# Two hyena gate tiles move into an attention head, where they share a seven-product pair

## The chip, the cores and the metric

The kernel runs on one core of a Trainium2 chip. The metric is the device time of one execution in microseconds. Three runs of the kernel before gave 885.85, 886.38 and 887.53 us, so a median of 886.38 us.

## What is computed

One layer of a hybrid backbone on 640 tokens (128 prompt tokens and 512 latent tokens) of 1024 channels, in float32. The modulated input `h` is multiplied by a wide projection `w_in`, whose columns feed two branches. Cut to what matters here:

```python
hy, g_h, qkv, g_a, m = split(h @ w_in)          # 3072, 1024, 3072, 1024, 2048 columns
v_h, x1, x0 = split(short_conv(hy))             # three groups of channels, three taps each
u   = v_h * x1
y_h = (irfft(rfft(u) * rfft(filter)) + u * d_bias) * x0        # hyena branch
y_a = attention(q, k, v)                                       # attention branch
p_h = (y_h * silu(g_h)) @ w_bh
p_a = (y_a * silu(g_a)) @ w_ba
out = (sigmoid(m_h) * p_h + sigmoid(m_a) * p_a) @ w_out
x_new = layer_norm(ALPHA * x + gate * out)
```

The change concerns `silu(g_h)` for the first 256 of the 1024 hyena channels. The kernel computes `silu(z)` as `(tanh(z/2) + 1) * z`; the missing factor 1/2 is taken into later constants.

## The kernel before

Everything is channel-major: a tile has 128 channels on the partitions and the 640 tokens along the free side, in two halves of 320. Every float32 matrix is split into a high part and a low part of the type fp32r, and a product is three matmuls (high by high, high by low, low by high). An output tile of 128 channels from 1024 inputs is therefore 8 blocks of inputs x 3 products x 2 halves = 48 matmuls of 320 columns (`proj`, `accumulate`, L168).

The program has these stages, in order of time:

1. Prologue: modulation, `h` in high and low parts (`hH`, `hL`), the filter network.
2. Hyena stage, in four quarters of two channel tiles (rows `n` = 2q and 2q+1). `quarter_head(q)` makes `v_h` and `x1` of the two rows, that is four projection tiles with their short convolution (`conv_tile`). `quarter_tail(q)` makes for each of the two rows a tile `x0` (`conv_tile`) and a gate tile `g_h` (`gate_tile`, weights 24 to 31). `long_conv` and `long_conv_back` do the transforms: small matmuls on TensorE with much VectorE work between them. `weave(main, side, n_main, n_side)` interleaves the projections (main) with the transforms and the next filter spectrum (side) in proportion to the two counts; one full quarter has eight projection tiles, `8 * NK` steps.
3. The row `yh` of the hyena branch is `silu(g_h) * x0 * u`. `gapped_product` multiplies and at the same time brings the token order of the convolution (image rows) into the order of the attention (column blocks). When both factors are there, `gate_conv` multiplies by `u` and stores the row to DRAM (`yh_d`).
4. Attention, eight pairs of heads `j` = 0 to 7 (called heads here). Each head has four steps of scores, softmax and values (`attend`), woven into projections for later heads (`mains`). From head 1 on these projections are made in pairs of output tiles by `pair_tile`: a two-by-two block product with seven instead of eight block multiplications, on sums of the weights (`prepare`, L1033) and sums of `h` (`token_sums`). A pair is 7 products x 4 blocks x 3 = 84 matmuls of 320 columns (L1068). `pair_tile` hands out the four quarters of the result in the order (1,1), (0,0), (1,0), (0,1), as (tile, half), by a callback `use`. `follow` says which pair's weights are prepared while a pair is computed. In head 1 the pairs are `mix(0)` and `queries_keys(3)`, in head 2 `mix(1)`, `queries_keys(4)` and `gates_a(2)`.
5. Output: the rows `yh` come back from DRAM (`yh_raw`, the first ones in head 7), are split, and go through `w_bh`, `w_ba`, the merge, `w_out` and the layer norm.

What sets the order: each engine runs its instructions in the order of its queue. In the attention stage TensorE's order is that of the program text. Everywhere else, and on the other engines throughout, a scheduler that plays the program on assumed durations chooses the order at build time. Loads are issued by SyncE's queue (`nc.sync`, SPq), some stores by ScalarE's (`nc.scalar`), and in the hyena stage the low part of a weight is made by an accumulating DMA from GpSimd's queue (L148). The ring of prepared weights `wb` has two buffers of one tag and three of another, raw weights have two.

Of the kernel before, what the change touches and what calls it, by code (L numbers as in the profile page):

```python
# [18 lines left out]
NK = 8  # L19
# [26 lines left out]
def tile_hyena_natten_step(ctx: ExitStack, tc: tile.TileContext, a, o):  # L46
# [424 lines left out]
    def gapped_product(y, x):  # L471
        nc.vector.tensor_tensor(y[:, :LP], y[:, :LP], x[:, :LP], op=ALU.mult)
        xs, yb = by_row(x[:, GAP:NG]), y[:, SC : SC + LS]
        for b0, n, src in ((0, 1, xs[:, :, 7:8]), (1, 7, xs[:, :, 0:7])):
            ys = from_blocks(yb[:, 64 * b0 : 64 * (b0 + n)], n)
            nc.vector.tensor_tensor(ys, ys, src, op=ALU.mult)

    def conv_tile(i, dst):
        lo, hi = yield from proj(i, eng="dma")
        convw = out["convw"]  # L480
        zs = zss[0]
        zss.reverse()
        nc.scalar.activation(zs[:, 1 : 1 + LP], lo[:, :LP], AF.Copy)
        nat = by_row(zs[:, GAP + 1 : NG + 1])
        nc.scalar.activation(nat[:, :, 7:8], from_blocks(lo[:, B7], 1), AF.Copy)
        nc.scalar.activation(nat[:, :, 0:2], from_blocks(lo[:, B01], 2), AF.Copy)
        nc.scalar.activation(nat[:, :, 2:7], from_blocks(hi[:, :HALF], 5), AF.Copy)
        d = dst[:, :NG]
# [40 lines left out]
    def quarter_tail(q):  # L529
        yh = out["yh"]  # L530
        for i in range(2):
            n = 2 * q + i
            x0 = hwa.tile([P, NG + 1], F32, tag="cv", bufs=2, name=f"x0_{n}")
            yield from conv_tile(16 + n, x0)
            yield
            yh[n] = row(yhp, "yh", f"yh{n}")
            yield from gate_tile(24 + n, yh[n][:], "dma")
            gapped_product(yh[n], x0)
            gate_conv(n)
            yield  # L540

# [132 lines left out]
    pinned[0] = False  # L674
    for q in range(3):
        weave(chain(quarter_head(q + 1), quarter_tail(q)), chain(long_conv(q), braid(long_conv_back(q), filter_spectrum(q + 1))),
              8 * NK, N_CONV + N_BACK + N_FILTER)
    ident = out["ident"]

    def rows(h):  # L680
# [371 lines left out]

    def pair_tile(i0, i1, use):
        def halfrow(tag, bufs, name):
            return sp.tile([P, 384], F32, tag=tag, bufs=bufs, name=f"{name}{i0}")[:, :HALF]

        if i0 not in ready:
            prepare(i0, i1, False)
        wb, prep = ready.pop(i0)
        ps = {}  # L1060
        for j in range(7):
            if j < 4:
                ps["xyvz"[j]] = acc(f"sp{i0}_{j}")[:, :HALF]
            dst, x = ps["xyvzxvz"[j]], operand(ORDER[j])
            for k in range(4):
                wh, wl = (wb[j][:, i, P * k : P * k + P] for i in range(2))
                for i, (wk, xi) in enumerate(((wh, 0), (wh, 1), (wl, 0))):
                    nc.tensor.matmul(  # L1068
                        dst, wk, x(xi, k), start=j < 4 and k == 0 and i == 0, stop=k == 3 and i == 2, skip_group_check=True,
                    )  # L1070
                if k == 1:
                    yield
            if j == 0:
                u = halfrow("u", 1, "u")
                nc.scalar.activation(u, dst, AF.Copy)
            elif j == 1:
                nc.vector.tensor_tensor(u, dst, u, op=ALU.add)
            elif j == 4:
                use(0, 0, dst)
            else:  # L1080
                if j != 3:
                    c = halfrow("c", 4, f"c{j}_")
                nc.vector.tensor_tensor(c, dst, c if j == 3 else u, op=ALU.add)
                if j != 2:
                    use(*{3: (1, 1), 5: (1, 0), 6: (0, 1)}[j], c)
            prep(j + 5)
            if j == 3 and (i0, i1) in follow:
                prepare(*follow[i0, i1], True)
            yield
# [5 lines left out]
    def gates_a(j):  # L1095
# [7 lines left out]

        yield from pair_tile(T_GA + j, T_GA + j + 1, use)

    def mix(m):
        t0, dst = (T_MH, mh_d) if m < 4 else (T_MA, ma_d)
        n0 = 2 * (m % 4)

        def use(i, hf, src):  # L1110
            th = sp.tile([P, 384], F32, tag="c", bufs=4, name=f"th{m}")[:, :HALF] if hf == i == 0 else src
# [13 lines left out]
    def mix_(m):  # L1125
        t = (T_MH if m < 4 else T_MA) + 2 * (m % 4)
        return t, t + 1

    runs = (
        (mix_(0), qk_(3), mix_(1), qk_(4), ga_(2)), (mix_(2), qk_(5), mix_(3), ga_(4), qk_(6)),  # L1130
        (mix_(4), qk_(7), mix_(5), ga_(6), mix_(6), mix_(7)),
    )
    follow = {x: y for run in runs for x, y in zip(run, run[1:])}
# [45 lines left out]
    def mains(j):  # L1179
        return {  # L1180
            0: ((alongside(chain(gate_a(1), queries(2), keys(2)), token_sums(1), 2, 5),), 3 * NK),
            1: ((mix(0), queries_keys(3)), 2 * N_PAIR),
            2: ((mix(1), queries_keys(4), gates_a(2)), 3 * N_PAIR),
            3: ((values(2), mix(2)), N_VALUES + N_PAIR),
            4: ((queries_keys(5), mix(3), gates_a(4)), 3 * N_PAIR),
# [327 lines left out]
```

## Time and profile before

| what | value |
|---|---|
| median of three runs | 886.38 us (885.85 to 887.53) |
| profiled execution: its time, and its span | 885.91 us, 884.1 us |
| TensorE (PE) busy, weight loads (PEld) busy | 872.7 us, 844.7 us |
| VectorE (DVE), ScalarE (ACT), GpSimd (POOL) busy | 635.2, 429.4, 127.4 us |
| granted TensorE clock | 0.997 of full speed on average |
| matmuls | 6532 |

A row of the group view gives the source line, the engine, the operation, the tile written and the tiles read, then the busy time and the mean duration of one, then the idle time of the engine just before it and what ended it. Matmuls overlap: one of 320 columns is shown as 310 ns long, though the next starts sooner. A row of the time line gives the start, the length and how many alike were merged. A row of the chain of waits gives the start, the length of the piece and what ran in it.

The attention stage begins near 387 us of the span and ends near 706 us.

### The profile page before, as it was taken

What the parts mean: (1) busy time and instruction counts of PE and PEld (TensorE: products, weight loads), DVE (VectorE), ACT (ScalarE), POOL (GpSimd) and SP (SyncE); (2) the same over time, 40 slices, a digit from 0 to 9 for tenths busy, and PEclk for the clock granted to TensorE, in tenths of its full rate; (3) what the DMA queues carried; (4) which work ended last, traced back from release to release, by engine and by line L of the source; (5) the groups of instructions that cost most, each with busy time, mean ns of one, the idle gap of its engine ahead of it and who ended that gap; (6) DMA issues with size and microseconds to landing.
All of it is one profiled execution on the core that took longest, in us unless ns stands there. A gap on an engine that the chain in (4) does not pass through costs nothing.

```text
span 884.1 us, 16779 instructions
## 1 busy us (share of the span) xinstructions
PE 872.7 (99%) x6532; PEld 844.7 (96%) x6532; DVE 635.2 (72%) x1257; ACT 429.4 (49%) x912; POOL 127.4 (14%) x128
## 2 busy tenths in 40 slices
PE   8999999999999999999999999999999999999996
PEld 7899999999999999999999999999999999999885
DVE  5776693795679478699787567865877667676666
ACT  4395454645445432356665465555655632243200
POOL 0010110010101000024423322222222200000000
PEclk9999999999999999999999999999999999999998
DMA  9975666656656231253525153434252488545611
GB/s 351 381 165 131 140 136 123 140 136 142 141 118 137 71 108 55 72 195 104 164 80 168 55 153 99 142 105 124 78 181 80 135 304 279 165 157 195 212 62 57
DMA packets 53834, 129.07 MB, mean 146 GB/s; under 512 B 8283, under 2 KB 23131, under 8 KB 53756
## 3 DMA queue, kind: packets, MB, share of 16 engines
q1 hardware_dynamic: 44108, 107.72, 37.4%
q0 software_dynamic: 4032, 14.68, 10.2%
q10 hardware_dynamic: 5616, 5.61, 1.9%
q8 instruction: 51, 0.84, 0.4%
q14 instruction: 27, 0.22, 0.1%
HBM read 113.83 MB, written 14.16 MB: 145 GB/s over the span
## 4 chain that ended last, share of the span: by engine, by line
PE 94%; DVE 3%; DMA 1%; ACT 1%; issue 0%; POOL 0%; POOLq 0%; DVEq 0%; ACTq 0%
PE mm L168 38%; PE sp L1068 19%; PE mm L182 6%; PE out L1328 6%; PE v L769 5%; PE pt L866 2%; PE s L873 2%; PE s L826 2%; PE ve L781 1%; DMA raw<-wall 1%; PE adaT L249 1%; DVE wb L102 1%; DVE s L1033 1%; PE adaT L266 1%; PE fl L401 1%; PE yb L158 1%
## 5 line engine op out<-in xcount | busy, mean ns | idle before, releaser
L1068 PE MATMUL sp<-t,wb 128*128 128x320 f32 x768 | 120.6, 310 | 0.0
L168 PE MATMUL mm<-hH,wh 128*128 128x320 f32 x480 | 114.6, 313 | 0.9 <-ACT hH L329 0.7
L1068 PEld LDWEIGHTS sp<-t,wb 128*128 128x128 f32 x768 | 113.8, 188 | 0.5 <-issue 0.5
L168 PE MATMUL mm<-hL,wh 128*128 128x320 f32 x480 | 113.0, 311 | 0.0
L168 PE MATMUL mm<-hH,wl 128*128 128x320 f32 x480 | 112.1, 310 | 0.4 <-DVE wl L102 0.4
L1068 PE MATMUL sp<-hH,wb 128*128 128x320 f32 x384 | 93.2, 313 | 0.0
L168 PEld LDWEIGHTS mm<-hH,wh 128*128 128x128 f32 x480 | 80.7, 188 | 3.3 <-issue 1.4
L168 PEld LDWEIGHTS mm<-hL,wh 128*128 128x128 f32 x480 | 80.9, 188 | 1.1 <-DVE hL L330 0.5
L168 PEld LDWEIGHTS mm<-hH,wl 128*128 128x128 f32 x480 | 80.8, 188 | 0.8 <-DVE wl L102 0.7
L1068 PEld LDWEIGHTS sp<-hH,wb 128*128 128x128 f32 x384 | 66.1, 188 | 1.9 <-issue 1.9
L101 ACT ACTIVATE wh<-raw 128x1024 fp32r<-128x1024 f32 x33 | 34.8, 1058 | 60.4 <-PE mm L168 29.1
L848 POOL TENSOR_SCALAR p<-p,sm 128x384 f32<-128x384 f32 x32 | 47.6, 1497 | 108.7 <-DVE sm L847 76.2
L148 POOL DMA_DIRECT2D wl<-wall x28 | 24.4, 871 | 259.3 <-ACT wl L147 232.2
L1068 PE MATMUL sp<-hL,wb 128*128 128x320 f32 x192 | 59.3, 309 | 0.0
L102 DVE TENSOR_TENSOR wb<-s,wb 128x512 fp32r<-128x512 f32 x64 | 43.7, 695 | 16.7 <-ACT wb L101 16.7
L149 ACT ACTIVATE wh<-raw 128x1024 fp32r<-128x1024 f32 x28 | 29.7, 1062 | 50.6 <-PE mm L168 50.6
L101 ACT ACTIVATE wb<-s 128x512 fp32r<-128x512 f32 x64 | 39.0, 628 | 30.0 <-DVE s L1033 24.5
L102 DVE TENSOR_TENSOR wl<-raw,wh 128x1024 fp32r<-128x1024 f32 x33 | 40.2, 1220 | 12.1 <-ACT wh L101 11.9
L1328 PE MATMUL out<-woh,yhs 128*128 128x512 f32 (+1 forms) x176 | 45.5, 372 | 0.0
L101 ACT ACTIVATE wb<-raw 128x512 fp32r<-128x512 f32 x48 | 30.1, 627 | 31.2 <-PE sp L1068 17.3
L848 POOL TENSOR_SCALAR edge<-edge,sm 128x320 f32<-128x320 f32 x32 | 43.6, 1373 | 1.9 <-DVE sm L847 1.9
L102 DVE TENSOR_TENSOR wb<-raw,wb 128x512 fp32r<-128x512 f32 x48 | 33.4, 697 | 12.6 <-ACT wb L101 11.7
(357 smaller groups left out, 2164.5 us busy)
## 6 DMA issues: line engine op xcount, KB each, us to landing
raw<-wall SPq DMA_DIRECT2D x95, 512.0 KB, 3.7
wl<-wall POOLq DMA_DIRECT2D x28, 512.0 KB, 5.6
ada<-wada SPq DMA_DIRECT2D x16, 512.0 KB, 8.3
tm<-bias SPq DMA_DIRECT2D x16, 512.0 KB, 4.5
gate<-wgate SPq DMA_DIRECT2D x8, 512.0 KB, 3.9
wo<-wall SPq DMA_DIRECT2D x8, 512.0 KB, 4.2
xt<-xT SPq DMA_DIRECT2D x8, 320.0 KB, 7.8
dec<-decay SPq DMA_DIRECT2D x20, 128.0 KB, 3.4
```

What stands on the lines that cost most here:

```text
L101: hi = nc.scalar.activation(dst_h, src, AF.Copy)
L102: return hi, (eng or nc.vector).tensor_tensor(dst_l, src, f(dst_h), op=ALU.subtract)
L148: nc.gpsimd.dma_start(wl, a["wall"][i], accum_op=ALU.add)
L149: nc.scalar.activation(wh, raw[:], AF.Copy)
L168: nc.tensor.matmul(ps[hf][:, :HALF], wt[k], x[:, hf * HALF : (hf + 1) * HALF], start=(i == 0 and k == 0), stop=(i == lead[2] and k == NK - ...
L182: nc.tensor.matmul(p[:, :HALF], w[i // 2][k], (hH, hL)[i % 2][:, k, cs], start=n == 0, stop=n == len(steps) - 1, skip_group_check=True,)
L769: nc.tensor.matmul(ps[t // 2][:, t % 2 * 256 : t % 2 * 256 + 256], x[:, k, P * t : P * t + P], wk, start=first and t % 2 == 0, stop=last, ...
L826: nc.tensor.matmul(dst[h], x[rows(h), qs], y[rows(h), ks], start=i == 0, stop=i == 2, skip_group_check=True)
L848: nc.gpsimd.tensor_scalar_mul(pv, pv, sm[:, 2:3])
L866: nc.tensor.transpose(pt[:, i * P : i * P + P], x, ident)
L1068: nc.tensor.matmul(dst, wk, x(xi, k), start=j < 4 and k == 0 and i == 0, stop=k == 3 and i == 2, skip_group_check=True,)
L1328: ins = nc.tensor.matmul(dst, m[k][:, c0 : c0 + P], w[:, c : c + n], start=(first and k == 0), stop=(last and k == 5), skip_group_check=True,)
```

## The change

- For rows 0 and 1, both of quarter 0, the gate tile leaves `quarter_tail`. In its place `natural` copies `x0` into the row in the new token order, three ScalarE copies. The row that `gate_conv` stores to `yh_d` is then `x0 * u`, without its gate.
- The two gate tiles are made together as one pair in head 1, after `mix(0)` and `queries_keys(3)`, by `gates_h`. Its callback takes each half row of 320 tokens from DRAM (two buffers, tag `yg`), multiplies it by `z`, makes `tanh(z/2)`, adds one and multiplies, and stores the half row to its place in `yh_d` from ScalarE's queue. The half rows three and four are fetched into the buffers of the first two after these have been stored.
- The main count of quarter 0's weave goes from 64 to 48 steps, that of head 1 from 28 to 42, and `follow` gets the new pair between `queries_keys(3)` and `mix(1)`.
- Half-row scratch tiles are 320 instead of 384 columns wide.

```diff
+    def natural(y, x):
+        nc.scalar.activation(y[:, :LP], x[:, :LP], AF.Copy)
+        xs, yb = by_row(x[:, GAP:NG]), y[:, SC : SC + LS]
+        for b0, n, src in ((0, 1, xs[:, :, 7:8]), (1, 7, xs[:, :, 0:7])):
+            nc.scalar.activation(from_blocks(yb[:, 64 * b0 : 64 * (b0 + n)], n), src, AF.Copy)
...
-            yield from gate_tile(24 + n, yh[n][:], "dma")
-            gapped_product(yh[n], x0)
+            if n in (0, 1):
+                natural(yh[n], x0)
+            else:
+                yield from gate_tile(24 + n, yh[n][:], "dma")
+                gapped_product(yh[n], x0)
...
-              8 * NK, N_CONV + N_BACK + N_FILTER)
+              (8 - sum(n // 2 == q for n in (0, 1))) * NK, N_CONV + N_BACK + N_FILTER)
...
-            return sp.tile([P, 384], F32, tag=tag, bufs=bufs, name=f"{name}{i0}")[:, :HALF]
+            return sp.tile([P, HALF], F32, tag=tag, bufs=bufs, name=f"{name}{i0}")[:]
...
+    def gates_h(*ns):
+        order = ((1, 1), (0, 0), (1, 0), (0, 1))
+        ys = {}
+
+        def fetch(k):
+            if k < 4:
+                i, hf = order[k]
+                ys[k] = at.tile([P, HALF], F32, tag="yg", bufs=2, name=f"yg{ns[i]}_{hf}")
+                nc.sync.dma_start(ys[k][:], yh_d[ns[i]][:, CS[hf]])
+
+        def use(i, hf, src):
+            k = order.index((i, hf))
+            y = ys[k][:]
+            th = sp.tile([P, HALF], F32, tag="c", bufs=4, name=f"gh{ns[0]}")[:] if hf == i == 0 else src
+            nc.vector.tensor_tensor(y, y, src, op=ALU.mult)
+            nc.scalar.activation(th, src, AF.Tanh, scale=0.5)
+            nc.vector.scalar_tensor_tensor(y, th, 1.0, y, op0=ALU.add, op1=ALU.mult)
+            nc.scalar.dma_start(yh_d[ns[i]][:, CS[hf]], y)
+            fetch(k + 2)
+
+        fetch(0)
+        fetch(1)
+        yield from pair_tile(24 + ns[0], 24 + ns[1], use)
...
-        (mix_(0), qk_(3), mix_(1), qk_(4), ga_(2)), (mix_(2), qk_(5), mix_(3), ga_(4), qk_(6)),
+        (mix_(0), qk_(3), gh_(0), mix_(1), qk_(4), ga_(2)), (mix_(2), qk_(5), mix_(3), ga_(4), qk_(6)),
...
-            1: ((mix(0), queries_keys(3)), 2 * N_PAIR),
+            1: ((mix(0), queries_keys(3), gates_h(*GH[0])), 3 * N_PAIR),
```

How the order moves. VectorE, before, where head 1 hands over to `mix(1)`, the first pair of head 2 (`wb` are prepared weights of `mix(1)`, `s` sums of raw weights, `kl` low parts of keys, `c` half rows of the pair's result):

```order
L102 TENSOR_TENSOR wb_2_5278<-s_66_5268,wb_2_5278 128x512
L1033 TENSOR_TENSOR s_66_5270<-raw_5264,s_66_5270 128x512
L741 TENSOR_TENSOR kl_5259<-c_35_5346,k_5258 128x64
L741 TENSOR_TENSOR kl_5259<-c_35_5346,k_5258 128x128
L1033 TENSOR_TENSOR s_66_5281<-raw_5266 128x512
L741 TENSOR_TENSOR kl_5259<-c_35_5346,k_5258 128x128
L1083 TENSOR_TENSOR c_35_5370<-sp_3_5244,u_5207 128x320
L102 TENSOR_TENSOR wb_4_5287<-raw_5264,wb_4_5287 128x512
L102 TENSOR_TENSOR wb_3_5284<-s_66_5281,wb_3_5284 128x512
```

The low parts of keys of `queries_keys(3)` stand between the weights of `mix(1)`; none of these instructions reads what a DMA has just fetched, but for the raw weights. VectorE at the same handover with the change (`yg` are the half rows fetched from DRAM, `smp` and `yo` belong to the attention step):

```order
L1092 TENSOR_TENSOR c_24_5401<-sp_3_5306,u_5245 128x320
L102 TENSOR_TENSOR wb_2_5340<-s_66_5330,wb_2_5340 128x512
L1042 TENSOR_TENSOR s_66_5332<-raw_5326,s_66_5332 128x512
L1129 TENSOR_TENSOR yg_0_5324<-yg_0_5324,c_24_5383 128x320
L102 TENSOR_TENSOR wb_4_5349<-raw_5326,wb_4_5349 128x512
L1042 TENSOR_TENSOR s_66_5343<-raw_5328 128x512
L1129 TENSOR_TENSOR yg_1_5369<-yg_1_5369,c_24_5401 128x320
L902 TENSOR_REDUCE smp_5457<-s_0_5414 128x1
L902 TENSOR_REDUCE smp_5457<-s_1_5415 128x1
L1131 SCALAR_TENSOR_TENSOR yg_0_5324<-c_24_5383,yg_0_5324 128x320
L923 TENSOR_TENSOR yo_5444<-sg_4388,s_0_5416 128x128
L102 TENSOR_TENSOR wb_3_5346<-s_66_5343,wb_3_5346 128x512
```

The products of the third and fourth half row (`yg_0_5324`, `yg_1_5369`), which wait for their fetch, now stand ahead of the weights `wb_4` and `wb_3` of `mix(1)`. SyncE's queue with the change, at that place:

```order
L748 DMA new_kT<-c_35_5200 128x128
L63 DMA tm_5487<-bias 128x1024
L63 DMA tm_5489<-bias 128x1024
L63 DMA raw_5326<-wall 128x1024
L63 DMA raw_5328<-wall 128x1024
L1123 DMA yg_0_5324<-yh_d 128x320
L1123 DMA yg_1_5369<-yh_d 128x320
L63 DMA raw_5550<-wall 128x1024
```

The two late fetches come behind the raw weights of `mix(1)` (5326, 5328) and ahead of those of `queries_keys(4)` (5550); before, two bias loads (`tm`) and one store stood between them. ScalarE in quarter 0 with the change, where before the gate's two `tanh` (L501) stood:

```order
L147 ACTIVATE wl_1817<-raw_1814 128x1024
L495 ACTIVATE x_1_1496<-zs_104,pack_373 128x641
L419 ACTIVATE F_1172<-fa_1173 128x2x256
L479 ACTIVATE yh_1482<-x_0_1357 128x128
L482 ACTIVATE yh_1482<-x_0_1357 128x64
L482 ACTIVATE yh_1482<-x_0_1357 128x8x7x8
L101 ACTIVATE sh_2_1207<-sd_2_1205 128x512
```

The three copies of `natural` (L479, L482) take the place of the two `tanh` and of one gate tile's two weight copies. From head 2's second pair on, the order on every engine is as before.

More of the change, by code (lines that the diff above doesn't have):

```diff
@@ L1110, in use @@
         def use(i, hf, src):
-            th = sp.tile([P, 384], F32, tag="c", bufs=4, name=f"th{m}")[:, :HALF] if hf == i == 0 else src
+            th = sp.tile([P, HALF], F32, tag="c", bufs=4, name=f"th{m}")[:] if hf == i == 0 else src
             nc.scalar.activation(th, src, AF.Tanh, scale=0.5)
@@ L1127, in mix_, with gh_ @@
         return t, t + 1
+    GH = ((0, 1), ())
+    def gh_(m):
+        return 24 + GH[m][0], 24 + GH[m][1]
     runs = (
-        (mix_(0), qk_(3), mix_(1), qk_(4), ga_(2)), (mix_(2), qk_(5), mix_(3), ga_(4), qk_(6)),
+        (mix_(0), qk_(3), gh_(0), mix_(1), qk_(4), ga_(2)), (mix_(2), qk_(5), mix_(3), ga_(4), qk_(6)),
         (mix_(4), qk_(7), mix_(5), ga_(6), mix_(6), mix_(7)),
```

## The prediction

> **What bounds the kernel now.** First the page's busy times, with the granted clock and the shares of the chain of waits that ended last.
>
> ```profile
> span 884.1 us, 16779 instructions
> PE 872.7 (99%) x6532; PEld 844.7 (96%) x6532; DVE 635.2 (72%) x1257; ACT 429.4 (49%) x912; POOL 127.4 (14%) x128
> PEclk9999999999999999999999999999999999999998
> PE 94%; DVE 3%; DMA 1%; ACT 1%; issue 0%; POOL 0%; POOLq 0%; DVEq 0%; ACTq 0%
> ```
>
> TensorE is busy 99% of the span at full clock and holds 94% of the chain. Busy alone can hide gaps, since matmuls overlap; so next the view of waits, TensorE's own, which is complete with these five rows.
>
> ```profile
> PE adaT L266 <- POOL spare L281: 1.5, 1, 1.5
> PE mm L168 <- ACT hH L329: 0.7, 1, 0.7
> PE mm L168 <- DVE wl L102: 0.4, 1, 0.4
> PE mm L168 <- ACT wh L101: 0.2, 1, 0.2
> PE adaT L249 <- DVE arg L219: 0.2, 1, 0.2
> ```
>
> That is 3.0 us, all in the prologue. Third, the chain in order of time (start, length, what), for what one matmul really costs in either place of the change: the length of a piece over its count is the distance between starts.
>
> ```profile
> 278.46 10.12 PE mm L168 x69
> 541.21 9.67 PE sp L1068 x66
> ```
>
> 10.12/69 and 9.67/66 give 146.7 and 146.5 ns: a projection matmul of 320 columns costs the same in the hyena stage (L168) and in a pair (L1068). Last, the stages that the change touches, by windows: quarters 0 and 1 of the hyena stage, head 1 and head 2.
>
> ```profile
> 83.00:164.00 81.00, 81.00 (x574) 80.54 (x573) 55.25 (x90) 43.75 (x82) 7.78 (x9) 1.00 0.62 135
> 164.00:244.00 80.00, 80.00 (x566) 79.54 (x565) 55.68 (x89) 42.81 (x82) 7.78 (x9) 1.00 0.61 134
> 411.30:445.00 33.70, 33.70 (x279) 32.52 (x278) 28.82 (x81) 23.00 (x65) 11.27 (x10) 1.00 0.41 131
> 445.00:491.00 46.00, 46.00 (x363) 44.82 (x362) 35.31 (x95) 28.01 (x69) 14.62 (x10) 1.00 0.43 129
> ```
>
> After each window's length come PE, PEld, DVE, ACT and POOL. TensorE is full in all four; VectorE, the next, has 55 of 81 us in quarter 0 and 29 of 34 in head 1. So what the change does to the number of matmuls is time, and what it does on the other engines is time only where a result comes too late for TensorE.
>
> **The change part by part.** *TensorE.* Two gate tiles leave: 2 x 48 = 96 matmuls. One pair comes: 84. The transforms, scores and values keep their counts, and so do the transposes that stand alone in the stream. The net is 12 matmuls less, 12 x 0.1467 = 1.76 us (14.08 out, 12.32 in).
>
> [...]
>
> *Other engines in quarter 0.* The durations:
>
> ```profile
> L147 ACT ACTIVATE wl<-raw 128x1024 fp32r<-128x1024 f32 x28 | 30.0, 1072 | 0.0
> L501 ACT ACTIVATE yh<-mm 128x320 f32<-128x320 f32 x16 | 6.0, 426 | 0.0
> L496 DVE SCALAR_TENSOR_TENSOR yh<-yh,mm 128x320 f32<-128x320 f32 x16 | 7.1, 480 | 0.0
> L476 DVE TENSOR_TENSOR yh<-yh,x 128x64 f32<-128x64 f32 (+1 forms) x16 | 6.3, 418 | 0.0
> L472 DVE TENSOR_TENSOR yh<-yh,x 128x128 f32<-128x128 f32 x8 | 2.3, 283 | 0.0
> ```
>
> VectorE loses four gate products and the two rows' products with x0: 4 x 0.48 + 4 x 0.42 + 2 x 0.28 = 4.2 us. ScalarE loses 4 weight copies (1.07 each) and 4 tanh, 6.0 us, and gains six small copies, bounded by the tanh at 0.43 each: 2.6 us. Two raw loads and two accumulating loads leave their queues, and come back as the pair's two raw loads. All of it lies beside TensorE, so I cost it at nothing. The cover: quarter 0 shrinks to 81 - 14.1 = 66.9 us, with 55.25 - 4.2 = 51 us of VectorE work, 76% against 68% before. The tight place is the spectrum product, where TensorE has only projections to run between the last matmul on `p_X` and the first on `yb`. By the order of instructions these are 163 with the change against 176 in quarter 0; quarter 1 got by with 139 before (20.4 us) and did not wait, and with the change quarters 1 and 2 have 152 and 164. Were the cover gone, each missing projection matmul would be 0.147 us of wait.
>
> *Other engines in head 1.* The pair's VectorE work, in rows of the same operations:
>
> ```profile
> L102 DVE TENSOR_TENSOR wb<-s,wb 128x512 fp32r<-128x512 f32 x64 | 43.7, 695 | 16.7 <-ACT wb L101 16.7
> L1033 DVE TENSOR_TENSOR s<-raw,raw 128x512 f32<-128x512 f32 x16 | 11.2, 703 | 8.2 <-DMA raw<-wall 8.2
> L1083 DVE TENSOR_TENSOR c<-sp,u 128x320 f32<-128x320 f32 x48 | 23.2, 484 | 13.6 <-PE sp L1068 13.6
> L496 DVE SCALAR_TENSOR_TENSOR sg<-sg,c 128x320 f32<-128x320 f32 x9 | 4.4, 485 | 0.5 <-ACT sg L1101 0.5
> ```
>
> Four sums and seven low parts (11 x 0.70), five result additions, four products and four gates (13 x 0.484): 14.0 us, brought by a pair that is 12.3 us on TensorE. Head 1 then has at most 28.8 + 14.0 = 42.8 us of VectorE work in 46.0 us, 93%: still under TensorE, so again nothing, as long as the order has no late place. The latest is the handover to `mix(1)`. Before, on VectorE's and TensorE's time lines:
>
> ```profile
> 443.84 0.68 DVE L102 TENSOR_TENSOR wb<-s,wb 128x512 fp32r<-128x512 f32 x1
> 444.44 0.69 DVE L1033 TENSOR_TENSOR s<-raw,s 128x512 f32<-128x512 f32 x1
> 446.18 0.48 DVE L1083 TENSOR_TENSOR c<-sp,u 128x320 f32<-128x320 f32 x1
> 446.58 0.68 DVE L102 TENSOR_TENSOR wb<-raw,wb 128x512 fp32r<-128x512 f32 x1
> 447.18 0.68 DVE L102 TENSOR_TENSOR wb<-s,wb 128x512 fp32r<-128x512 f32 x1
> 445.73 0.31 PE L1068 MATMUL sp<-hH,wb 128*128 128x320 f32 x1
> 448.92 0.42 PE L1068 MATMUL sp<-hH,wb 128*128 128x320 f32 x1
> 449.90 5.43 PE L1068 MATMUL sp<-t,wb 128*128 128x320 f32 x36
> ```
>
> The last of the VectorE rows is `wb_3`, the weights of product 3, ready at 447.86; product 3 is the third dozen of the 36 and begins at 449.90 + 24 x 0.1467 = 453.42. The cushion is 5.6 us. VectorE's starts are 0.60 us apart for 512 columns and 0.40 for 320.
>
> With the change I count from T, the end of the gate pair's product 3 (the first quarter handed out). VectorE adds (to T+0.6), multiplies (1.1), makes `wb_0` (1.7), multiplies the second quarter, whose product ends at T+1.76 (2.4), and gates the first (2.8). Now the first half row goes out, and the third comes back into its buffer. The nearest rows for these two transfers:
>
> ```profile
> mh_d<-c ACTq DMA_DIRECT2D x12, 160.0 KB, 1.8
> dec<-decay SPq DMA_DIRECT2D x20, 128.0 KB, 3.4
> ck<-ck SPq DMA_DIRECT2D x8, 64.0 KB, 2.3
> yhraw<-yh_d SPq DMA_DIRECT2D x8, 320.0 KB, 3.9
> ```
>
> The store has its like: 1.8. The fetch of 160 KB lies between 2.3 and 3.9, and I take the 3.4 of the nearest size. So the third half row is there at T + 2.9 + 1.8 + 3.4 = T+8.1 (7.0 to 8.6). VectorE reaches its product at about T+7.2 and waits 1.0 us (0 to 1.4). Behind it in its queue are `wb_4`, a sum, the fourth product (fetched by then), two reductions, a gate, one `yo` and `wb_3`, which ends at about T+11.9. TensorE wants `wb_3` after the pair (T+5.3), 36 matmuls (5.3) and the scores and values between (448.92 - 445.88 = 3.0): T+13.6. Cushion 1.7 us, thinner than 5.6, but there: no wait. That a VectorE wait of this size need not reach TensorE is seen in head 1 itself, where this one left TensorE full:
>
> ```profile
> 423.95 0.69 DVE L1033 TENSOR_TENSOR s<-raw,raw 128x512 f32<-128x512 f32 x1 [1.62 <-DMA raw<-wall]
> ```
>
> The first two fetches stand early in SyncE's queue and wait for stores made two hundred microseconds before; the four stores of ScalarE delay nothing that has under 2 us to spare. Both cost nothing.
>
> *Sum.* The profiled execution took 885.91 us, 884.1 of it span; minus 1.76 gives 884.15. It lies 0.47 below the median of the runs, so on that: 886.38 - 1.76 = **884.6 us**. I call 0.2%, 1.77 us, what a measurement of this kernel can tell from no change. The forecast sits on that line.
>
> **The rivals.** (1) *The handover eats part of the gain.* For: the cushion is 1.7 us, and other rows of stores and loads are longer:
>
> ```profile
> ma_d<-th ACTq DMA_DIRECT2D x4, 160.0 KB, 2.8
> yaraw<-ya_d SPq DMA_DIRECT2D x8, 320.0 KB, 5.6
> ada<-wada SPq DMA_DIRECT2D x16, 512.0 KB, 8.3
> ```
>
> 2.8 + 5.6 = 8.4 against the assumed 5.2 makes `wb_3` 3.2 later, 1.5 past the cushion: 884.6 + 1.5 = 886.1. Against: they are of other stages, and the rows nearest by stage and size are the 1.8 and the 3.4.
>
> (2) *Slower: the late fetch blocks VectorE for so long that TensorE stands.* The same place, but with 2.8 + 8.3 = 11.1 for the round trip: 5.9 later, 4.2 us of wait for TensorE, 884.6 + 4.2 = 888.8. It decides from a round trip of 5.2 + 1.7 = 6.9 us on, and makes the kernel slower by 0.2% from 10.4 us on. For: nothing behind the product can pass it. Against: the 8.3 is of loads three times as large, and in head 1 the DMA engines are busy 0.41 of the time.
>
> [...]
>
> (3) *More than the matmuls.* Head 1's attention steps will stand 60 instead of 42 projection matmuls apart, and the weight loads show 1.2 us in which they were not busy in its 33.7. If half a microsecond of such gaps closes: 884.1. Against: head 2 has that spacing already, and the same 1.2.
>
> That the change does not do what it says is excluded by the order: 96 and 84 are there.
>
> **How the numbers follow.** Full gain (884.6) 0.60, part eaten (886.1) 0.18, slower (888.8) 0.12, more (884.1) 0.10. The first splits evenly over the 0.2% line; the last is faster, the second no change. Faster 0.30 + 0.10 = 0.40, within 0.2% 0.30 + 0.18 = 0.48, slower 0.12. The range goes from half a microsecond under the third rival, 883.6, over the first rival and into the second's lower part, 887.6.
>
> **What would show it.** Right: matmul count 12 lower, TensorE's waits still five rows of 3.0 us, quarter 0 about 67 us long, head 1 about 46, span 882.3. Rival 1 or 2: a row in which a pair's matmul (L1068 before) waits for VectorE's `wb`, and a row in which VectorE's product with `yg` waits for the DMA from `yh_d`. The forecast is wrong if TensorE waits in the quarters after the prologue, which I hold to be covered, or if the fetch is over 6.9 us behind its store's issue.

## The result, and the profile after

Six runs of the changed kernel gave 890.76 to 893.21 us, median **891.94 us**; six of the kernel before, on the same chips, 885.82 to 887.53, median 886.36. The ratio is 1.0063, with a 95% interval of 1.0053 to 1.0073: the change costs 5.6 us. Forecast were 884.6 us and a gain. The profiled execution took 891.75 us, 889.8 of it span; before, 885.91 and 884.1.

The page of the kernel after: busy times, the granted clock in forty slices, and the shares of the chain of waits.

```profile
span 889.8 us, 16796 instructions
PE 874.7 (98%) x6520; PEld 845.3 (95%) x6520; DVE 644.1 (72%) x1271; ACT 432.3 (49%) x922; POOL 124.6 (14%) x126
PEclk9999999999899999999999999999999999999999
PE 92%; DVE 4%; DMA 2%; ACT 1%; issue 0%; POOL 0%; POOLq 0%; SPq 0%; ACTq 0%; DVEq 0%
```

The matmuls are the 12 fewer that were forecast, and yet TensorE is busy 2.0 us longer. The row of the clock says why: the eleventh slice has an 8 where the kernel before had a 9. TensorE's share of the chain fell from 94% to 92%. Next TensorE's own waits (total, times, longest):

```profile
PE fp L156 <- ACT sh L101: 2.4, 1, 2.4
PE mm L168 <- ACT zs L492: 0.6, 1, 0.6
PE y L653 <- DVE sd L407: 0.3, 1, 0.3
PE pt L875 <- DVE sm L850: 0.2, 1, 0.2
```

These four are new beside the five of the prologue (and one more of 0.2 us in the attention). The first three lie in the hyena stage: `y` at 147.8 us, and `fp` and `mm` within 3 us of each other, at 233.90 and 236.57. Two windows of 5 us there; the last three columns are the granted clock, the DMA share and GB/s:

```profile
230.00:235.00 5.00, 2.59 (x15) 2.25 (x13) 5.00 (x10) 4.02 (x7) 0.86 (x1) 0.89 0.60 215
235.00:240.00 5.00, 4.33 (x17) 3.71 (x16) 5.00 (x9) 4.55 (x13) 0.00 (x0) 0.50 0.81 156
```

Both together have 32 matmuls; at 0.147 us between starts, the distance of 320-column ones, 10 us would hold 68. In the second window TensorE is counted busy for 4.33 of 5 us, but at a granted clock of 0.50. VectorE is busy for all of both. On the time line (start, length, engine, line, what; in brackets how long the engine stood and for whom):

```profile
229.18 0.93 ACT L495 ACTIVATE u<-zs,pack 128x641 f32<-128x641 f32 x1 [5.70 <-DVE yh L476]
229.77 0.39 PE L402 MATMUL fl<-w3l,hid 128*128 128x512 f32 x1
230.90 0.71 DVE L446 TENSOR_TENSOR F<-F,fc 128x512 f32<-128x512 f32 x1
231.03 0.45 PE L168 MATMUL mm<-hH,wl 128*128 128x320 f32 x2
231.50 0.91 DVE L497 SCALAR_TENSOR_TENSOR u<-zs,pack,u 128x641 f32<-128x641 f32 x1
232.29 0.71 DVE L407 TENSOR_TENSOR sd<-fl,dec 128x512 f32<-128x512 f32 x1
233.23 0.62 ACT L101 ACTIVATE sh<-sd 128x512 fp32r<-128x512 f32 x1
233.90 0.58 PE L156 MATMUL fp<-sh,dftH 128*128 128x256 f32 x1 [2.41 <-ACT sh L101]
236.57 0.64 PE L168 MATMUL mm<-hH,wh 128*128 128x320 f32 x1 [0.62 <-ACT zs L492]
239.14 0.47 PE L168 MATMUL mm<-hH,wl 128*128 128x320 f32 x1
239.41 0.47 PE L168 MATMUL mm<-hH,wh 128*128 128x320 f32 x1
241.05 0.31 PE L168 MATMUL mm<-hL,wh 128*128 128x320 f32 x1
241.19 0.31 PE L168 MATMUL mm<-hH,wh 128*128 128x320 f32 x1
```

Read it from the middle. TensorE made the last part of the next filter, `fl`, at 229.77. The product behind it on VectorE, `sd`, came only at 232.29, behind other work of VectorE's queue (the last two pieces are the rows `F` and `u`); its high part `sh` at 233.23; and the transform `fp` that needs it at 233.90. Between `fl` and `fp` TensorE had nine projection matmuls, and the last two began at 231.03. I take it that the scheduler had no more to put there because the next rows are held up too: the copy into a buffer of `u` at 229.18 had waited 5.70 us for the product of `yh` that reads an older `u`. Before, 53 projection matmuls stood between the same two rows, and nothing waited:

```profile
236.06 0.40 PE L402 MATMUL fl<-w3l,hid 128*128 128x512 f32 x1
244.07 0.28 PE L156 MATMUL fp<-sh,dftH 128*128 128x256 f32 x1
```

Behind the wait the starts of 320-column matmuls are 0.27 us apart (239.14 to 239.41) instead of 0.147; at 241.05 they are back. From 231.18, the start of the second of those two, to 240.74 TensorE did in 9.56 us what takes about 3.1 at full clock (an estimate from the distances between starts elsewhere: 12 projection matmuls of 0.147 us, seven matmuls of 256 columns and four transposes at 0.12): 6.4 us lost, about 3 by standing and 3.4 by the slow clock.

### The profile page after: what moved, and what is told of

Its sections match the earlier page's. It is cut to its first block, busy times and chain, and to the rows that moved or that the text cites. A ratio compares the mean times of both kernels' runs of the same rounds, so it can differ in the third digit from the quotient of the medians.

```text
span 889.8 us, 16796 instructions
## 1 busy us (share of the span) xinstructions
PE 874.7 (98%) x6520; PEld 845.3 (95%) x6520; DVE 644.1 (72%) x1271; ACT 432.3 (49%) x922; POOL 124.6 (14%) x126
## 4 chain that ended last, share of the span: by engine, by line
PE 92%; DVE 4%; DMA 2%; ACT 1%; issue 0%; POOL 0%; POOLq 0%; SPq 0%; ACTq 0%; DVEq 0%
PE mm L168 36%; PE sp L1077 20%; PE mm L182 6%; PE out L1366 6%; PE v L778 5%; PE pt L875 2%; PE s L882 2%; PE s L835 2%; PE ve L790 1%; DMA raw<-wall 1%; PE adaT L249 1%; DVE wb L102 1%; PE adaT L266 1%; PE yb L158 1%; PE yb L156 1%; PE fl L401 1%
## 5 line engine op out<-in xcount | busy, mean ns | idle before, releaser
L1077 PE MATMUL sp<-t,wb 128*128 128x320 f32 x816 | 128.5, 310 | 0.0
L1077 PEld LDWEIGHTS sp<-t,wb 128*128 128x128 f32 x816 | 120.9, 188 | 0.5 <-issue 0.5
L168 PE MATMUL mm<-hH,wh 128*128 128x320 f32 x448 | 109.2, 315 | 1.5 <-ACT hH L329 0.7
L168 PE MATMUL mm<-hL,wh 128*128 128x320 f32 x448 | 108.5, 311 | 0.0
L168 PE MATMUL mm<-hH,wl 128*128 128x320 f32 x448 | 107.8, 311 | 0.4 <-DVE wl L102 0.4
L1077 PE MATMUL sp<-hH,wb 128*128 128x320 f32 x408 | 98.4, 312 | 0.0
L168 PEld LDWEIGHTS mm<-hH,wh 128*128 128x128 f32 x448 | 76.1, 189 | 4.0 <-issue 1.4
L168 PEld LDWEIGHTS mm<-hL,wh 128*128 128x128 f32 x448 | 77.0, 189 | 0.9 <-DVE hL L330 0.5
L168 PEld LDWEIGHTS mm<-hH,wl 128*128 128x128 f32 x448 | 76.5, 189 | 1.2 <-DVE wl L102 0.7
L1077 PEld LDWEIGHTS sp<-hH,wb 128*128 128x128 f32 x408 | 70.1, 188 | 1.9 <-issue 1.9
```

Source lines behind the costliest of these rows:

```text
L168: nc.tensor.matmul(ps[hf][:, :HALF], wt[k], x[:, hf * HALF : (hf + 1) * HALF], start=(i == 0 and k == 0), stop=(i == lead[2] and k == NK - ...
L1077: nc.tensor.matmul(dst, wk, x(xi, k), start=j < 4 and k == 0 and i == 0, stop=k == 3 and i == 2, skip_group_check=True,)
```

## The experiments

For each run one number says what it lost beside its matmuls: the span of its profiled execution, less 884.1 us corrected for the matmuls taken out or added, at 0.1467 us. With the change 889.8 - (884.1 - 1.76) = 7.5 us. A profiled execution is one of several: that of chain_three, 888.07 us, was the longest of its ten, whose median is 886.65, so its 3.8 is too high by about 1.4. The run five_filled is left out of the table, since its added matmuls have another size.

| run | span | matmuls against before | lost beside them |
|---|---|---|---|
| before | 884.1 | 0 | 0 |
| short_before | 884.3 | 0 | 0.2 |
| five_before | 884.4 | 0 | 0.3 |
| one_row | 879.8 | -48 | 2.7 |
| hy_half | 877.5 | -96 | 7.5 |
| at_half | 896.2 | +84 | -0.2 |
| the change | 889.8 | -12 | 7.5 |
| rows_0_6 | 894.9 | -12 | 12.6 |
| rows_2_4 | 893.2 | -12 | 10.9 |
| u_five | 892.1 | -12 | 9.8 |
| low_on_pool | 890.6 | -12 | 8.3 |
| side_work_out | 887.8 | -12 | 5.5 |
| chain_three | 886.1 | -12 | 3.8 |
| short_after | 885.1 | -12 | 2.8 |
| same_load | 884.5 | -12 | 2.2 |
| five_short | 882.9 | -12 | 0.6 |

### The two halves apart

**hy_half** makes only the half in the hyena stage (the pair is left out of `runs` and `mains`, so rows 0 and 1 stay ungated); **at_half** only the half in head 1 (quarter 0 keeps its gates, so the two rows are gated twice).

First hy_half, then at_half, each against the kernel after:

```diff
-        (mix_(0), qk_(3), gh_(0), mix_(1), qk_(4), ga_(2)), (mix_(2), qk_(5), mix_(3), ga_(4), qk_(6)),
+        (mix_(0), qk_(3), mix_(1), qk_(4), ga_(2)), (mix_(2), qk_(5), mix_(3), ga_(4), qk_(6)),
...
-            1: ((mix(0), queries_keys(3), gates_h(*GH[0])), 3 * N_PAIR),
+            1: ((mix(0), queries_keys(3)), 2 * N_PAIR),
```

```diff
-            if n in (0, 1):
-                natural(yh[n], x0)
-            else:
-                yield from gate_tile(24 + n, yh[n][:], "dma")
-                gapped_product(yh[n], x0)
+            yield from gate_tile(24 + n, yh[n][:], "dma")
+            gapped_product(yh[n], x0)
...
-              (8 - sum(n // 2 == q for n in (0, 1))) * NK, N_CONV + N_BACK + N_FILTER)
+              8 * NK, N_CONV + N_BACK + N_FILTER)
```

> The hyena half of the change alone: the gates of rows 0 and 1 leave quarter 0, and the pair in head 1 is left out, so rows 0 and 1 stay without their gate. 96 matmuls less than before, 14.1 us. Theory (the loss lies in the hyena stage: the removed matmuls were cover for the chain of transforms, and TensorE waits at the end of quarter 1 and then runs on a lowered clock): the hyena stage gives about 7.1 of the 14.1 us, so 886.4 - 7.1 = 879.3 us, with the same wait of the filter's matmul for ScalarE near 231 us. Rival (the loss lies at the handover of head 1): 886.4 - 14.1 = 872.3 us.

> The attention half alone: the pair in head 1 is added, the gates of rows 0 and 1 stay in quarter 0 as well, so these two rows are gated twice. 84 matmuls more than before, 12.3 us. Theory (loss in the hyena stage): 886.4 + 12.3 + 0.5 = 899.2 us, no wait in the hyena stage and full clock. Rival (loss at the handover): 886.4 + 12.3 + 7 = 906 us, with waits of a pair's matmuls for the weights.

Measured: hy_half 879.48 us (ratio 0.9922, 0.9906 to 0.9939), at_half 898.58 (1.0135, 1.0119 to 1.0150). Taking out 14.1 us of matmuls gained 7.3; putting 12.3 us in cost 11.8 to 12.1, and TensorE had no wait but the prologue's. By the spans the loss is wholly in the hyena stage (7.5 and -0.2 us in the table). By the medians the two halves add up to 4.5 us of loss, against 5.6 for the change; the intervals, about 1.4 us each way for either half, allow both. hy_half has the same 2.4 us wait of `fp` as the change. The handover to `mix(1)`, on which two of the prediction's rivals rest, costs nothing: at_half has this handover too, and no wait in it.

### How much may leave, and from where

**one_row** takes only row 0's gate out (left ungated, no pair); **rows_0_6** and **rows_2_4** make the change for the rows that they name. Here is what sets the rows in one_row; in the others the same two lines have (0, 6) or (2, 4), and so has the pair in `GH`. The edit of one_row leaves the pair out of `runs` and `mains` as hy_half's does.

```diff
-            if n in (0, 1):
+            if n in (0,):
...
-              (8 - sum(n // 2 == q for n in (0, 1))) * NK, N_CONV + N_BACK + N_FILTER)
+              (8 - sum(n // 2 == q for n in (0,))) * NK, N_CONV + N_BACK + N_FILTER)
```

> Only the gate of row 0 leaves the hyena stage, and it is made nowhere (row 0 is left ungated, the pair is left out): 48 matmuls, 7.0 us, out of the kernel before. Theory (the chain of transforms through the four quarters ends at about 373 us whatever the matmuls do, some 7 us before TensorE's own work ended in the kernel before): up to 7 us can be gained, so this one gets nearly all of it, 879.4 to 880.5, hardly more than the two rows did (879.5), and TensorE waits 1 us or less after the prologue. Rival (each matmul taken out is paid back by half, evenly): 882.9.

> The same change for rows 0 and 6 in place of 0 and 1: one gate tile leaves quarter 0 and one leaves quarter 3, none of the quarters loses two. Same number of matmuls as in the change. Theory (TensorE can run ahead by about two projection tiles before the next quarter's buffers stop it, so one tile may leave without a wait): 884.6 us, TensorE's waits back to the five of the prologue, clock full. Rival (any projection that leaves the hyena stage is paid back, since the chain of transforms sets the pace there): the same loss as the change, near 892 us.

> The change made for rows 2 and 4, one tile out of quarter 1 and one out of quarter 2. Nothing is left out. By the order of instructions 25, 42, 28 and 16 projection matmuls stand between each quarter's last filter matmul and the next first transform (25, 25, 9 and 45 with rows 0 and 1). Theory (the chain has room for about 7 of the 14 us, so it does not matter from where they are taken): 890 to 896, TensorE waits at the end of the stage (368 to 377 us). Rival (only a place with few projections costs time, 16 is enough): 884.6 to 886.5.

Measured: one_row 881.85 us (ratio 0.9950, 0.9936 to 0.9965), between its two expectations; rows_0_6 896.08 (1.0106, 1.0091 to 1.0121); rows_2_4 895.30 (1.0103, 1.0088 to 1.0118). TensorE's new waits over 0.3 us in one_row:

```profile
PE fp L157 <- DVE sl L102: 1.5, 1, 1.5
PE mm L168 <- ACT zs L492: 0.8, 1, 0.8
```

In rows_0_6 the same two, and one more:

```profile
PE mm L182 <- ACT v L785: 4.8, 1, 4.8
PE fp L157 <- DVE sl L102: 1.5, 1, 1.5
PE mm L168 <- ACT zs L492: 0.8, 1, 0.8
```

And in rows_2_4:

```profile
PE mm L182 <- ACT v L785: 4.2, 1, 4.2
PE fp L157 <- DVE sl L102: 1.8, 2, 1.7
PE fp L156 <- ACT sh L101: 0.4, 1, 0.4
```

So even one tile, 7.0 us, is not free: 4.6 us are gained. That fells what I expected of rows_0_6, that one tile of a quarter may leave without a wait; its result lies above the rival's 892 too. rows_2_4 came out inside its theory's range of 890 to 896, with its wait where that theory put it. Still the room is not a fixed 7 us, as I wrote for one_row and rows_2_4: one_row lost 2.7 us of its 7.0, and rows_2_4, with the same matmuls taken out as the change, lost 10.9 where the change lost 7.5. It depends on the place. Spread over two quarters the loss is larger, because TensorE then comes early to the end of the stage as well. It stands there, at about 372 us, with a projection of the attention (L182) for ScalarE's copy into `v` (L785).

### The buffers of u

**u_five** gives `u` a fifth buffer and takes for it one of the two buffers of the tag `sd`, which holds the filter weights `w3` (not the product `sd` of the time line above); **five_before** does it to the kernel before. Two other tiles of the tag `u` get the new count as well; these lines are left out here.

```diff
-            u = hw.tile([P, NG + 1], F32, tag="u", bufs=4, name=f"u{n}")
+            u = hw.tile([P, NG + 1], F32, tag="u", bufs=5, name=f"u{n}")
...
-        pre[q] = hwa.tile([P, 512], F32, tag="sd", bufs=2, name=f"w3_{q}")
+        pre[q] = hwa.tile([P, 512], F32, tag="sd", bufs=1, name=f"w3_{q}")
```

> The change as it is, with five instead of four buffers for the rows u; to make room the filter weights w3 have one buffer instead of two. Theory (the next quarter's first rows u cannot be written before the quarter's transforms have given their buffers back, ScalarE stands in front of that write, and TensorE's banks stay full behind it): the wait near 231 us goes, the clock stays, 884.6 us, at most 886. Rival (VectorE is too full in the shortened quarter, whatever the buffers): 891 to 892 us.

> Control: the kernel before with five buffers for u and one for sd. Theory (before, TensorE has cover everywhere): 886.4, no wait after the prologue. Rival (the one buffer of sd, or the space, costs time by itself): 888 or more, with a wait that also lies in u_five.

Measured: u_five 893.71 us (ratio 1.0081, 1.0066 to 1.0096), five_before 886.51 (1.0002, 0.9993 to 1.0011). The waits near 231 us are gone in u_five: between `fl` and `fp` of that filter it has 42 projection matmuls in place of nine. So the buffers had their part in them; but the time is not back, neither the theory nor the rival was right. Its time line:

```profile
367.30 1.04 PE L653 MATMUL y<-pack,ye 128*128 128x128 f32 x8
372.89 1.42 DVE L476 TENSOR_TENSOR yh<-yh,u 128x64 f32<-128x64 f32 x4
374.43 1.08 ACT L785 ACTIVATE v<-v 128x512 f32<-128x512 f32 x2 [1.83 <-DVE yh L476]
375.08 0.64 PE L182 MATMUL mm<-hH,wh 128*128 128x320 f32 x1 [6.75 <-ACT v L785]
```

Two windows there, with the granted clock third from the end:

```profile
370.00:375.00 5.00, 0.00 (x0) 0.00 (x0) 5.00 (x12) 1.31 (x3) 0.40 (x4) 0.86 0.10 39
375.00:380.00 5.00, 4.92 (x18) 4.92 (x19) 4.85 (x11) 2.58 (x10) 0.00 (x0) 0.50 0.99 316
```

TensorE is through with the last transposes `y` at 368 us, ahead of everything else, and stands 6.75 us: the copy into `v` waits for the last products of `yh` (372.89 to 374.31). One wait was exchanged for a later and longer one.

### The chain made shorter

**short_after** and **short_before** leave three VectorE operations on the spectrum out of every quarter, in the changed kernel and in the one before; **five_short** is short_after with u_five's buffers.

```diff
-        nc.vector.tensor_tensor(X[:], X[:], F[:], op=ALU.mult)
         yield
         R = out[f"R{q}"] = X
         out[f"W{q}"] = W
-        nc.vector.tensor_tensor(R[:, 0:5], X[:, 0:5], X[:, 5:10], op=ALU.subtract)
-        nc.vector.tensor_tensor(R[:, 5:10], W[:, 0:5], W[:, 5:10], op=ALU.add)
```

> The changed kernel with a shorter chain: in every quarter the product of the whole spectrum with the filter, the difference and the sum behind it are left out (2.82 + 1.48 + 1.49 us of VectorE in each, 23 us in all; so the convolution's values are not the reference's). No matmul is touched. Theory (the chain is the second bound): TensorE's waits near 231 us and their slow clock are gone, 884.6, at most 886. Rival (the time comes from the matmul order or from buffers, not from the length of the chain): 891 to 892, as in the changed kernel.

> Control: the kernel before with the same three operations left out of every quarter. Theory (there TensorE covers the chain): no change, 886.4. [...]

> The changed kernel with five buffers for u and with the chain shortened as in short_after (three operations on the spectrum left out of every quarter, so the convolution's values are not the reference's). Theory (the two walls, the buffers of u near 231 us and the end of the chain at 368 to 375 us, are all that the change ran into): no wait over 0.5 us between 83 and 390 us, 884.6. Rival (less cover costs more than these two): 886.5 or more.

Measured: short_after 886.55 us (ratio 1.0000, 0.9991 to 1.0009), short_before 886.14 (0.9999, 0.9990 to 1.0009), five_short 885.27 (0.9985, 0.9975 to 0.9994). With less to do in each quarter the changed kernel gives back 5.4 us; the kernel before does not become faster beyond its interval. short_after lies half a microsecond above the theory's 886 and keeps two waits, of 1.4 us at `c_X` in quarter 1 and of 1.2 us in the attention; five_short keeps none, only the prologue's five rows, and its span is 882.9 us. That is the 882.3 that the prediction wanted, to 0.6, though with work left out.

**low_on_pool** tries to shorten the chain with nothing left out: the filter's low parts go from VectorE to GpSimd.

```diff
-            split(sh[:], sl[:], sd[:])
+            split(sh[:], sl[:], sd[:], nc.gpsimd)
```

> The changed kernel, complete, with the low parts of the filter's rows (L102, called at L410: five per quarter, 0.69 us each on VectorE) made by GpSimd, which is 14% busy. Theory: VectorE's queue loses 3.4 us per quarter, the chain is shorter if GpSimd's operation is not much over 2 us (its row of 384 columns takes 1.47, so about 2.0 for 512): 884.6 to 887. Rival (GpSimd's longer operations lengthen the filter's chain by 1.3 us a step): 892 or more.

Measured: 891.81 us (ratio 1.0060, 1.0045 to 1.0075), as the change and as the rival said. GpSimd took 1.96 us for a low part, VectorE 0.69. The waits are others: `fa` and `fp` now wait for GpSimd's low parts, 1.7 and 0.9 us.

```profile
PE fa L157 <- POOL sl L102: 1.7, 1, 1.7
PE fp L157 <- POOL sl L102: 0.9, 1, 0.9
```

### Length of the chain, or load of VectorE?

short_after took away both. **side_work_out** takes load away beside the chain (two taps of the x0 rows), **chain_three** shortens quarters 0 to 2 alone, and **same_load** is chain_three with the left-out work done elsewhere, for nothing.

First side_work_out, then what same_load adds at the end of `long_conv_back`:

```diff
-        for c in (0, 2):
+        for c in (0, 2) if i < 16 else ():
```

```diff
+        if q < 3:
+            nc.vector.tensor_tensor(R[:], R[:], W[:], op=ALU.mult)
+            nc.vector.tensor_tensor(R[:, 0:5], R[:, 0:5], R[:, 5:10], op=ALU.subtract)
+            nc.vector.tensor_tensor(R[:, 5:10], W[:, 0:5], W[:, 5:10], op=ALU.add)
```

> The changed kernel with less VectorE work beside the chain: the two outer taps of the short convolution of the eight x0 tiles are left out (16 operations of 0.88 us, 14.1 us of VectorE in all, so x0 is not the reference's); x0 is wanted only by the last product of a row, the chain of transforms does not use it. No matmul is touched. Theory (the length of the chain decides, step behind step): little is gained, 890.5 to 892. Rival (VectorE's load decides, whatever the work is): 14.1 of the 23.2 us that short_after left out, so 14.1/23.2 of its 5.4 us, 888.7.

> As short_after, but the three operations on the spectrum are left out of quarters 0 to 2 only (17.4 us of VectorE; the convolution's values of these rows are not the reference's). Theory: what ran late near 231 us is what these quarters made late, so 886 to 887, as short_after. Rival (the last quarter's end decides): a wait at 366 to 376 us and 889 or more.

> As chain_three, but the same 17.4 us of VectorE are done after all, behind the last row of each quarter, on the quarter's own dead tiles and for nothing (the convolution's values of quarters 0 to 2 are not the reference's): VectorE's load is that of the changed kernel, the chain of a quarter is 5.8 us shorter. Theory (the length of the chain decides): 886 to 888, near chain_three. Rival (VectorE's load decides): 891 to 892, as the changed kernel.

Measured: side_work_out 889.51 us (ratio 1.0037, 1.0024 to 1.0050), chain_three 886.65 (1.0002, 0.9992 to 1.0012), same_load 886.36 (1.0005, 0.9996 to 1.0014). One window over the whole stage (PE, PEld, DVE, ACT, POOL, clock, DMA share, GB/s), in the kernel after:

```profile
83.00:387.00 304.00, 300.65 (x2151) 297.34 (x2151) 220.88 (x364) 150.69 (x298) 20.94 (x29) 0.99 0.49 119
```

In same_load:

```profile
83.00:387.00 304.00, 302.62 (x2190) 300.20 (x2189) 228.24 (x376) 153.59 (x307) 26.30 (x31) 1.00 0.49 121
```

In side_work_out:

```profile
83.00:387.00 304.00, 301.94 (x2171) 298.85 (x2170) 210.49 (x351) 149.25 (x299) 22.51 (x30) 0.99 0.49 120
```

And of side_work_out's waits:

```profile
PE fp L157 <- DVE sl L102: 1.9, 1, 1.9
```

same_load has more VectorE work in these 304 us than the change, 228 against 221 us, and loses 2.2 us where the change loses 7.5; side_work_out has less, 210, and still waits 1.9 us at `fp`. (The windows end at the same time, but not at the same place: a faster run has more of the attention in them. Over the whole span VectorE is busy 645.5 us in same_load, 644.1 with the change, 631.3 in side_work_out.) So it is the length of the chain that decides, not VectorE's load. But the load is not nothing: side_work_out got 2.4 us back, and its interval, some 1.1 us each way, holds the rival's 888.7 and the theory's 890.5 alike. Work beside the chain can count where it stands ahead of a step of the chain in VectorE's queue, as at 230 to 232 us above.

What each run did at the place that waited can be counted on the time lines: the projection matmuls between the last `fl` and the first `fp` of quarter 2's filter, and the wait there. The change and hy_half have 9 and wait 2.4 us; side_work_out has 24 (1.9 us), low_on_pool 27 (0.9), rows_2_4 28 (1.7), one_row and rows_0_6 29 (1.5). With 42 (u_five, short_after, chain_three, same_load), 53 (before, at_half) or 58 (five_short) nothing waits. The number that is needed is not the same everywhere: at quarter 1's filter 25 were enough with the change. These counts also show a limit of the experiments: the scheduler chose a new order for each of them, so the chain's length and the order that follows from it were not changed separately. Order alone need not cost anything: short_before has another order too (48, 42 and 39 at the filters of quarters 1 to 3, against 42, 53 and 45 before), and the same time.

### Filling the wait

**five_filled** is u_five with 48 idle matmuls where TensorE stood, to see whether standing is what lowers the clock.

```diff
             gate_conv(n)
+            if n == NK - 1:
+                idle = aux("idle")
+                for _ in range(48):
+                    nc.tensor.matmul(idle[:, :256], dftH[:, 1, 0, 0, :], dftH[:, 1, 0], start=True, stop=True, skip_group_check=True)
```

> The kernel with five buffers for u, with 48 matmuls more on TensorE whose result nobody reads, at the place where it stood for 6.9 us (behind the last transposes back, 368.1 us): at 0.118 us for 256 columns they are 5.7 us, and end before the wait does. Nothing is left out. Theory (a TensorE that stands lowers its own clock afterwards, which cost about 2.4 us there): the matmuls cost nothing, starts stay 0.147 us apart behind the wait, 893.7 - 2.4 = 891.3. Rival (the clock falls for what runs then, not for the wait before): 893.7. Rival (the wait is for something that the added matmuls hold up): up to 893.7 + 5.7 = 899.4.

Measured: 899.01 us (ratio 1.0142, 1.0127 to 1.0157), the number of the second rival, but by another way. The time line:

```profile
368.26 5.99 PE L662 MATMUL idle<-dftH 128*128 128x256 f32 x48
374.09 0.31 PE L182 MATMUL mm<-hH,wh 128*128 128x320 f32 x1
374.24 0.31 PE L182 MATMUL mm<-hL,wh 128*128 128x320 f32 x1
```

And from the view of waits one that u_five does not have:

```profile
PE sp L1081 <- ACT wb L101: 3.6, 1, 3.6
```

At this place the theory held: behind the filled wait the granted clock is 1.00 (366 to 380 us, where u_five has 0.50 from 375 on) and the starts are 0.147 us apart, against 0.267 in u_five, and the next place that both share (the second projection tile behind the wait) is reached at 377.61 instead of 381.13 us. Of these 3.5 us the clock makes 2.5 (24 starts in 3.52 us instead of 6.05, where 2.4 was expected), the other 1.0 is that the first of them began at 374.09 instead of 375.08. Then it is lost: at 413 us a pair's matmul waits 3.6 us for its weights. The last low part of `token_sums` on VectorE ran at 408.66 us, 4.1 later than in u_five, and ScalarE's copies of the weight sums into `wb` at 412.55, 6.4 later; I take it that the scheduler put them later because of the added matmuls. That was not separated further, so the run prices the clock at its own place only.

## Why the prediction was wrong

- *Matmuls, 12 fewer at 0.1467 us.* Right in count (6520 against 6532), and in time as far as it can be seen: at_half's span is 12.1 us longer where 12.3 were set, and five_short, with the chain out of the way, is 1.2 us shorter than before where 1.76 were set. No run shows the 14.1 us of the hyena stage by themselves.
- *Head 1, costed at nothing.* Right. VectorE was busy 39.09 of the 46 us where at most 42.8 were counted, and TensorE full, as the window of head 1 in the kernel after shows (its first pair begins at 404.2 us):

```profile
404.00:450.00 46.00, 46.00 (x362) 44.82 (x361) 39.09 (x102) 27.84 (x75) 11.46 (x10) 1.00 0.39 125
```

- *Rivals 1 and 2, the late half row.* They did not come. VectorE's third product with `yg` has no wait behind its row on the time line of the kernel after:

```profile
452.45 0.48 DVE L1129 TENSOR_TENSOR yg<-yg,c 128x320 f32<-128x320 f32 x1
```

  It did not stand for its fetch; the stores and fetches there landed 1.8 to 2.5 us after their issue, so the round trip was 5.0 us at most where I had set 5.2. That the second forecast slower, and the result was slower, is no credit to it: nothing waited at its place.
- *Quarter 0, costed at nothing.* **This step failed.** The prediction said "All of it lies beside TensorE, so I cost it at nothing", and gave VectorE's 76% and the 163 projection matmuls between `p_X` and `yb` as the cover. Cover was there, and nothing waited in that place. Nor did quarter 0 shrink to 67 us: the scheduler spread the missing matmuls over two quarters. From one filter's first `fp` to the next, quarter 0 went from 433 to 389 projection matmuls and from 80.7 to 74.7 us, quarter 1 from 430 to 384 and from 80.4 to 76.2 us, quarter 2 only from 417 to 411; VectorE was busy 67% of the first stretch and 69% of the second, as before (68% and 70%). But the place between `p_X` and `yb` is only one of a chain that goes through all four quarters: transform, product with the filter, transform back, rows free their `u`, the next rows and the next filter start. The filter's own step, from `fl` to `fp`, has no place in the prediction. By the order of instructions its four occurrences had 25, 42, 53 and 45 projection matmuls before, and 25, 25, 9 and 45 with the change: the cover is thinnest at the filter of quarter 2, which is made at the end of quarter 1, a quarter behind the edit. The stream before that place stayed full but for 0.3 us. So taking the projections out made no hole at the edit; it brought TensorE forward until it ran into the chain. What the step left out, costed at nothing, measured 7.5 us of span.
- *The price of missing cover.* "0.147 us of wait for each missing projection matmul" was too low as well. It leaves out the clock (0.50 from 235 to 240 us): 7.5 us were lost though the five new waits add up to 3.7.
- *What would make it wrong.* The sentence that the forecast falls "if TensorE waits in the quarters after the prologue" named the right place, without a chance or a price of its own. The low probability of "slower" came from one rival in the wrong stage.

No complete version faster than the kernel before came out of this. The most that any run of the trade gained is five_short's 1.2 us of span, and it leaves work out.

## What to carry to other kernels

That an engine is busy 99% of the time tells nothing of how far the next bound is: its work is also the cover of a chain beside it. Before taking work out of such a stage, ask how long the chain would take without it: follow it through all repetitions, and count the cover at each of its steps by the order of instructions, also behind the edit, where the edit's missing work may turn up once a scheduler has moved it. If the chain has a few microseconds to spare, only these can be gained (here 7.3 of 14.1 us), while what is put back elsewhere costs its full price (12.1 us).

## What the runs showed of the hardware

After waits of 2.4 us (the change) and 6.75 us (u_five) TensorE's granted clock was lower for nearly 7 us: the window from 235 to 240 us has 0.50 in the change, that from 375 to 380 us 0.50 in u_five. That the standing makes it is shown at one place, where five_filled filled u_five's wait and kept the full clock (1.00 from 366 to 380 us). The starts of 320-column matmuls were then 0.267 us apart instead of 0.147 (u_five from 375.51 to 379.24 us, side_work_out from 236.71 to 239.64, after a wait of 1.9 us). After single waits of 1.5 us (one_row), 1.4 (short_after) and 1.7 (rows_2_4) the clock stayed at 1.00. But in low_on_pool TensorE stood only 1.3 us of the 5 us from 235 to 240, 0.9 of it in one wait, and the clock was 0.91 there and 0.75 from 240 to 245 us. So no one length of a wait separates the runs with the drop from those without.

In the trace's record of the granted clock, before and in the change, the drops lie a whole number of steps of 3.413 us behind the clock's first rise to 1.00. Before there is one, near the end of the span, 873.81 us behind the rise (256 steps); in the change there are two, 228.69 us (67 steps, the one at 233.9 us of the span) and 880.64 us (258, near the end). The slow stretch in the hyena stage is 6.83 us long in the change, two steps. For the other runs an estimate from the windows of 5 us (what their clock lacks of 1.00, if it was 0.50 in the slow part) gives 3.4 us in side_work_out, hy_half and low_on_pool, near one step, and 6.8 to 6.9 us in u_five, rows_0_6 and rows_2_4, near two. So when a wait falls may matter as well as how long it is; that was not settled.
